# Row skewness of a 1024 x 8192 array: fixed engine orders, new column widths and slices, moved copies and closing steps

## The chip, the cores and the metric

The kernel runs on one core of one Trainium2 chip. The metric is the device time of one execution in microseconds (us). The core has a matrix engine (TensorE, PE in the profile, with PEld for its weight loads), a vector engine (VectorE, DVE), a scalar engine (ScalarE, ACT), GpSimd (POOL) and SyncE (SP), which here only issues the transfers. Each engine runs its own list of instructions in order, and waits on semaphores for the others.

## The reference

```python
rows, cols = 1024, 8192            # x is float32, standard normal
mean = np.mean(x, axis=-1, keepdims=True)
std = np.std(x, axis=-1, keepdims=True)
z = (x - mean) / (std + 1e-8)
return np.mean(z ** 3, axis=-1).astype(np.float32)
```

For each row the third standardised moment is wanted. Both kernels get it from three sums over the row, of x, x^2 and x^3: with m1, m2, m3 the means of these, var = m2 - m1^2 and skew = (m3 - 3 m1 m2 + 2 m1^3) * var^-1.5.

## The kernel before

The 1024 rows are eight blocks of 128 partitions (block b takes rows p*8+b). A block of 8192 columns is cut into units, one load each; `UNITS` lists their widths block by block. The loads are issued by SP in the order of the units, through a pool of eight buffers (`xp`, tag `x`), so load i+8 waits until unit i has been used by every engine.

A unit is cut into slices of at most `SUB_MAX` = 2304 columns (`_slices`). For each slice:

- ScalarE squares it (L147, scale 8192^-0.5) into a tile `sq` and sums the squares into a column of `s2u`.
- VectorE multiplies `sq` by x (L152), and sums the cubes into a column of `s3u`. Four buffers of `sq` rotate.
- For the last unit of the last block the squares go to PSUM (`sqps`) and the products to `cube`.

Sums of x go by TensorE: each 128 x 128 piece of the unit is multiplied with an identity and accumulated into one PSUM tile `tp` (L165). At the end of the block ScalarE copies `tp` to SBUF (`tsb`, L174), and one product with a vector of ones (L175) gives the means in a column of `s1ps`. In blocks 0 to 2 ScalarE sums 1024 of the columns itself (L159).

Closing: after block 5, `close_first_blocks` computes skew of blocks 0 to 5, with two reductions on VectorE (L99), four small steps on ScalarE and six on GpSimd (L110 to L115). For blocks 6 and 7, `close_on_act` does it on ScalarE: it sums the block's columns of `s2u` there (L123), takes m1^2, the variance, -3 m1 and their product (L124 to L128), and puts the correction into a spare column of `s3u`. Its steps for block 6 stand between the first Squares of block 7. At the very end GpSimd raises both variances to -1.5 (L187), VectorE reduces the columns of `s3u` of both blocks (L189), multiplies (L192), and SP stores `skew` (L193).

The order of the instructions on each engine is set by a scheduler from the program, and here it follows the order in which they are written, but for a few small steps of the closings, which it puts elsewhere.

Of the kernel before, what the change touches and what calls it, by code (L numbers as in the profile page):

```python
# [8 lines left out]
FP = mybir.dt.float32  # L9
AF = mybir.ActivationFunctionType  # L10
ALU = mybir.AluOpType
X_AXIS = mybir.AxisListType.X


UNITS = [
    [4096, 4096],
    [4096, 4096],
    [4096, 4096],
    [4096, 4096],
    [3584, 2304, 2304],  # L20
    [2304, 2304, 2048, 1536],
    [1664, 1792, 1920, 1664, 1152],
    [1024, 1024, 1152, 1280, 1408, 1152, 1152],
]
S1_ACT = {(0, 0): 1024, (1, 0): 1024, (2, 0): 1024}
SUB_MAX = 2304
X_BUFS = 8
SQ_BUFS = 4
EARLY = 6


def _slices(w):
    n = -(-w // SUB_MAX)
    step = -(-w // n // 128) * 128
    return [(s, min(s + step, w)) for s in range(0, w, step)]


@with_exitstack
def kernel(
    ctx: ExitStack,  # L40
    tc: tile.TileContext,
    x: bass.AP,
    out: bass.AP,
):
    nc = tc.nc
    P = nc.NUM_PARTITIONS
    R, C = x.shape
    NB = R // P
    L = NB - 1
    F = EARLY  # L50
    inv_n = 1.0 / float(C)
    s_scale = float(C) ** -0.5
    third = (1.0 / 3.0) ** 0.5
    assert len(UNITS) == NB and all(sum(u) == C for u in UNITS)
    nw = len(S1_ACT)
    assert sorted(b for b, _ in S1_ACT) == list(range(nw)) and nw <= F


    xv = x.rearrange("(p b) c -> b p c", b=NB)
    ov = out.rearrange("(p b) -> p b", b=NB)  # L60


    K = max(sum(len(_slices(w)) for w in u) for u in UNITS) + 1

    xpool = ctx.enter_context(tc.tile_pool(name="xp", bufs=X_BUFS))
    sqpool = ctx.enter_context(tc.tile_pool(name="sqp", bufs=SQ_BUFS))
    onep = ctx.enter_context(tc.tile_pool(name="onep", bufs=1))
    psum = ctx.enter_context(tc.tile_pool(name="ps", bufs=2, space=bass.MemoryType.PSUM))
    psum1 = ctx.enter_context(tc.tile_pool(name="ps1", bufs=1, space=bass.MemoryType.PSUM))

    def small(name, n):
        return onep.tile([P, n], FP, tag=name, name=name)

    onesn = small("onesn", 1)
    nc.vector.memset(onesn, inv_n)  # L75
    tiny = small("tiny", 1)
    nc.scalar.activation(out=tiny, in_=onesn, func=AF.Square)  # L77
    ident = small("ident", P)
    make_identity(nc, ident)
    s2u = small("s2u", NB * K)  # L80
    s3u = small("s3u", NB * K)
    nc.vector.memset(s2u, 0.0)
    nc.vector.memset(s3u, 0.0)
    s1a = small("s1a", nw)
    same = small("same", max(S1_ACT.values()))
    junk = small("junk", K)
    expo = small("expo", F)
    nc.gpsimd.memset(expo, -1.5)
    skew = small("skew", NB)
    s1ps = psum1.tile([P, NB], FP, tag="s1ps")  # L90
    m1a = small("m1a", F)
    var2 = small("var2", NB - F)
    Tsb = [small(f"tsb{i}", P) for i in range(2)]

    def close_first_blocks():

        m2, m3 = small("m2a", F), small("m3a", F)
        for dst, src in ((m2, s2u), (m3, s3u)):
            nc.vector.tensor_reduce(  # L99
                out=dst, in_=src[:, 0 : F * K].rearrange("p (b c) -> p b c", c=K),  # L100
                axis=X_AXIS, op=ALU.add,
            )
        m1sq, m1sq3, nm1 = small("m1sqa", F), small("m1sq3a", F), small("nm1a", F)
        nc.scalar.copy(out=m1a[:, nw:F], in_=s1ps[:, nw:F])
        nc.scalar.activation(out=m1sq, in_=m1a, func=AF.Square)
        nc.scalar.activation(out=m1sq3, in_=m1a, func=AF.Square, scale=third)
        nc.scalar.activation(out=nm1, in_=m1a, func=AF.Copy, scale=-3.0)
        g = nc.gpsimd
        var, rr = small("vara", F), small("rra", F)
        g.tensor_tensor(out=var, in0=m2, in1=m1sq, op=ALU.subtract)  # L110
        g.tensor_tensor(out=m1sq3, in0=m1sq3, in1=var, op=ALU.add)  # L111
        g.tensor_tensor(out=m1sq3, in0=m1sq3, in1=nm1, op=ALU.mult)  # L112
        g.tensor_tensor(out=m3, in0=m3, in1=m1sq3, op=ALU.add)  # L113
        g.tensor_tensor(out=rr, in0=var, in1=expo, op=ALU.pow)  # L114
        g.tensor_tensor(out=skew[:, 0:F], in0=m3, in1=rr, op=ALU.mult)  # L115

    def close_on_act(b):

        m2, m1sq, nm1, v3 = (small(f"{t}_{b}", 1) for t in ("m2", "m1sq", "nm1", "v3"))
        p1 = s1ps[:, b : b + 1]  # L120
        var = var2[:, b - F : b - F + 1]
        act = nc.scalar.activation
        yield act(out=junk, in_=s2u[:, b * K : b * K + K], func=AF.Copy, accum_out=m2)  # L123
        yield act(out=m1sq, in_=p1, func=AF.Square)  # L124
        yield act(out=var, in_=m1sq, func=AF.Identity, scale=-1.0, bias=m2)  # L125
        yield act(out=nm1, in_=p1, func=AF.Copy, scale=-3.0)  # L126
        yield act(out=v3, in_=m1sq, func=AF.Identity, scale=1.0 / 3.0, bias=var)  # L127
        yield act(  # L128
            out=s3u[:, b * K + K - 1 : b * K + K], in_=v3, func=AF.Identity, scale=nm1
        )  # L130

    pending = iter(())
    for b, widths in enumerate(UNITS):
        tp = psum.tile([P, P], FP, tag="tp", name=f"tp_{b}")
        c0 = 0
        j = b * K
        for k, w in enumerate(widths):
            last_unit = b == L and k == len(widths) - 1
            xt = xpool.tile([P, w], FP, tag="x", name=f"x_{b}_{k}")
            nc.sync.dma_start(out=xt, in_=xv[b, :, c0 : c0 + w])  # L140
            c0 += w
            for s, e in _slices(w):
                if last_unit:
                    sq = psum1.tile([P, e - s], FP, tag="sqps", name=f"sqps_{s}")
                else:
                    sq = sqpool.tile([P, e - s], FP, tag="sq", name=f"sq_{b}_{k}_{s}")
                nc.scalar.activation(  # L147
                    out=sq, in_=xt[:, s:e], func=AF.Square, scale=s_scale,
                    accum_out=s2u[:, j : j + 1],
                )  # L150
                cube = sqpool.tile([P, e - s], FP, tag="sq", name="cube") if last_unit else sq
                nc.vector.scalar_tensor_tensor(  # L152
                    out=cube, in0=sq, scalar=1.0, in1=xt[:, s:e],
                    op0=ALU.mult, op1=ALU.mult, accum_out=s3u[:, j : j + 1],
                )
                j += 1
            w_act = S1_ACT.get((b, k), 0)
            if w_act:
                nc.scalar.activation(  # L159
                    out=same[:, 0:w_act], in_=xt[:, w - w_act : w], func=AF.Copy,  # L160
                    scale=inv_n, accum_out=s1a[:, b : b + 1],
                )
            n = (w - w_act) // P
            for c in range(n):
                nc.tensor.matmul(  # L165
                    out=tp, lhsT=xt[:, c * P : (c + 1) * P], rhs=ident,
                    start=(k == 0 and c == 0), stop=(c0 == C and c == n - 1),
                    is_transpose=True,
                )
            if k > 0:  # L170
                next(pending, None)
                next(pending, None)
        tsb = Tsb[b % 2]
        nc.scalar.copy(out=tsb, in_=tp)  # L174
        nc.tensor.matmul(out=s1ps[:, b : b + 1], lhsT=tsb, rhs=onesn, start=True, stop=True)  # L175
        if b == F - 2:
            nc.vector.tensor_tensor(
                out=m1a[:, 0:nw], in0=s1ps[:, 0:nw], in1=s1a, op=ALU.add
            )
        if b == F - 1:  # L180
            close_first_blocks()
        if b >= F:
            pending = close_on_act(b)
    for _ in pending:
        pass
    rr = small("rr2", NB - F)
    nc.gpsimd.tensor_tensor(out=rr, in0=var2, in1=expo[:, 0 : NB - F], op=ALU.pow)  # L187
    num = small("num2", NB - F)
    nc.vector.tensor_reduce(  # L189
        out=num, in_=s3u[:, F * K :].rearrange("p (b c) -> p b c", c=K), axis=X_AXIS, op=ALU.add  # L190
    )
    nc.vector.tensor_tensor(out=skew[:, F:NB], in0=num, in1=rr, op=ALU.mult)  # L192
    nc.sync.dma_start(out=ov, in_=skew)  # L193


# [28 lines left out]
```

## Time and profile before

| | |
|---|---|
| median of 8 runs | 91.67 us (91.54 to 91.89) |
| the profiled execution, its own time | 91.63 us |
| its span, first to last instruction | 89.9 us |
| busy: VectorE, ScalarE, PE, GpSimd | 72.9, 72.1, 64.5, 10.3 us |
| data read | 33.55 MB, 373 GB/s over the span |
| loads of x | 27, of 512 KB to 2 MB |

The profile is of one execution. In strips, a digit is the busy share in tenths of one of 40 equal slices of the span. In the chain, the columns are start, length, and what ran, with "issue" for time in which nothing that is shown was waited for. Rows of the timeline give start, length, engine, line, operation, output <- inputs, shapes, count, and in brackets the idle time before and what ended it. A wait's numbers are the total, how often, and the longest.

### The profile page before, as it was taken

To read this page: it belongs to the slowest core of one execution; us is meant where nothing else is said; L and a number is where in the kernel's file an instruction comes from. 1 tells how busy PE (TensorE), PEld (TensorE's weight loads), DVE (VectorE), ACT (ScalarE), POOL (GpSimd) and SP (SyncE) were. 2 spreads that over 40 slices of the span, in tenths; PEclk is the share of its full clock that TensorE was granted. 3 is DMA by queue.
4 is the path that set the end of the run, shared out by engine and by line. 5 is a ranking of instruction groups with operands and counts; after the bars stand their busy time and mean duration, and the time that the engine had idled before them with its cause. 6 is when DMAs were issued, how large, how long until landed. Compare 5 with 4: busy or idle time off the path is not lost.

```text
span 89.9 us, 1368 instructions
## 1 busy us (share of the span) xinstructions
PE 64.5 (72%) x504; PEld 58.7 (65%) x504; DVE 72.9 (81%) x80; ACT 72.1 (80%) x106; POOL 10.3 (11%) x14
## 2 busy tenths in 40 slices
PE   0002999692898919889598988888988798969710
PEld 0003999591896909778596977877876786848500
DVE  1000498989989298998989999999999999999970
ACT  6003999699991999979598989978979898999950
POOL 3000000000000000000000000000005999400030
PEclk9999999999669999999999999999999999999995
DMA  4899999999999999999999999999999999994000
GB/s 117 328 394 452 445 423 416 445 430 416 452 423 408 445 430 408 445 430 423 428 397 422 414 435 410 419 419 420 413 410 420 407 409 417 421 409 173 0 0 2
DMA packets 4038, 33.64 MB, mean 374 GB/s; under 512 B 576, under 2 KB 576, under 8 KB 2240
## 3 DMA queue, kind: packets, MB, share of 16 engines
q1 hardware_dynamic: 4032, 33.56, 89.8%
q8 instruction: 4, 0.07, 0.3%
q14 instruction: 2, 0.02, 0.0%
HBM read 33.55 MB, written 0.00 MB: 373 GB/s over the span
## 4 chain that ended last, share of the span: by engine, by line
DMA 74%; ACT 15%; issue 4%; DVE 2%; SPq 1%; PE 1%; ACTq 0%; DVEq 0%
DMA x<-in_x_dram 74%; ACT sq L147 11%; ACT sqps L147 1%; DVE sq L152 1%; ACT same L159 1%; SPq L140 1%; PE s1ps L175 1%; ACT tsb L174 0%; ACT s3u L128 0%; ACT v L127 0%; ACT var L125 0%; DVE num L189 0%; ACT m1sq L124 0%; DVE skew L192 0%; ACT nm L126 0%
## 5 line engine op out<-in xcount | busy, mean ns | idle before, releaser
L152 DVE SCALAR_TENSOR_TENSOR sq<-sq,x 128x2048 f32<-128x2048 f32 (+9 forms) x35 | 70.8, 2071 | 13.3 <-ACT sq L147 13.2
L165 PE MATMUL tp<-ident,x 128*128 128x128 f32 x488 | 62.0, 286 | 17.8 <-DMA x<-in_x_dram 17.6
L165 PEld LDWEIGHTS tp<-ident,x 128*128 128x128 f32 x488 | 57.0, 149 | 21.6 <-DMA x<-in_x_dram 13.1
L147 ACT ACTIVATE sq<-x 128x2048 f32<-128x2048 f32 (+9 forms) x35 | 60.6, 1733 | 11.4 <-DMA x<-in_x_dram 11.3
L110 POOL TENSOR_TENSOR vara<-m2a,m1sqa 128x6 f32<-128x6 f32 x1 | 1.8, 1825 | 67.0 <-DVE m3a L99 67.0
L147 ACT ACTIVATION_READ_ACCUMULATOR sq<-x 128x1 f32 x35 | 6.5, 185 | 0.0
L175 PEld LDWEIGHTS s1ps<-onesn,tsb 128*128 128x128 f32 x16 | 2.4, 188 | 5.3 <-ACT tsb L174 5.3
L175 PE MATMUL s1ps<-onesn,tsb 128*128 128x1 f32 x16 | 3.1, 260 | 3.4 <-ACT tsb L174 3.4
L174 ACT COPY tsb<-tp 128x128 f32<-128x128 f32 x8 | 2.0, 253 | 1.5 <-PE tp L165 1.5
L159 ACT ACTIVATE same<-x 128x1024 f32<-128x1024 f32 x3 | 3.1, 1041 | 0.0
L152 DVE DVE_READ_ACCUMULATOR sq<-sq,x 128x1 f32 x35 | 2.9, 82 | 0.0
L111 POOL TENSOR_TENSOR m1sq3a<-m1sq3a,vara 128x6 f32<-128x6 f32 x1 | 1.9, 1867 | 0.1
L77 ACT ACT_TABLE_LOAD x1 | 1.3, 1283 | 0.7 <-PEq L208 0.7
L113 POOL TENSOR_TENSOR m3a<-m3a,m1sq3a 128x6 f32<-128x6 f32 x1 | 1.7, 1737 | 0.1
L187 POOL TENSOR_TENSOR rr<-var,expo 128x2 f32<-128x2 f32 x1 | 0.7, 700 | 8.8 <-ACT var L125 8.8
L152 DVE SCALAR_TENSOR_TENSOR cube<-sqps,x 128x1152 f32<-128x1152 f32 x1 | 1.4, 1351 | 0.0
L114 POOL TENSOR_TENSOR rra<-vara,expo 128x6 f32<-128x6 f32 x1 | 1.3, 1333 | 0.0
L115 POOL TENSOR_TENSOR skew<-m3a,rra 128x6 f32<-128x6 f32 x1 | 1.2, 1198 | 0.1
L147 ACT ACTIVATE sqps<-x 128x1152 f32<-128x1152 f32 x1 | 1.1, 1137 | 0.1
L112 POOL TENSOR_TENSOR m1sq3a<-m1sq3a,nm1a 128x6 f32<-128x6 f32 x1 | 1.0, 981 | 0.0
L124 ACT ACTIVATE m1sq<-s1ps 128x1 f32<-128x1 f32 x2 | 0.3, 171 | 0.5 <-PE s1ps L175 0.5
L75 DVE MEMSET onesn<- 128x1 f32 x1 | 0.1, 59 | 0.8 <-PEq L208 0.8
(28 smaller groups left out, 6.7 us busy)
## 6 DMA issues: line engine op xcount, KB each, us to landing
x<-in_x_dram SPq DMA_DIRECT2D x8, 2048.0 KB, 23.5
x<-in_x_dram SPq DMA_DIRECT2D x4, 1152.0 KB, 27.9
x<-in_x_dram SPq DMA_DIRECT2D x4, 576.0 KB, 8.7
x<-in_x_dram SPq DMA_DIRECT2D x1, 1792.0 KB, 33.0
x<-in_x_dram SPq DMA_DIRECT2D x2, 832.0 KB, 14.1
x<-in_x_dram SPq DMA_DIRECT2D x1, 1024.0 KB, 21.1
x<-in_x_dram SPq DMA_DIRECT2D x2, 512.0 KB, 10.2
x<-in_x_dram SPq DMA_DIRECT2D x1, 960.0 KB, 13.4
```

What stands on the lines that cost most here:

```text
L77: nc.scalar.activation(out=tiny, in_=onesn, func=AF.Square)
L110: g.tensor_tensor(out=var, in0=m2, in1=m1sq, op=ALU.subtract)
L111: g.tensor_tensor(out=m1sq3, in0=m1sq3, in1=var, op=ALU.add)
L113: g.tensor_tensor(out=m3, in0=m3, in1=m1sq3, op=ALU.add)
L114: g.tensor_tensor(out=rr, in0=var, in1=expo, op=ALU.pow)
L115: g.tensor_tensor(out=skew[:, 0:F], in0=m3, in1=rr, op=ALU.mult)
L147: nc.scalar.activation(out=sq, in_=xt[:, s:e], func=AF.Square, scale=s_scale, accum_out=s2u[:, j : j + 1],)
L152: nc.vector.scalar_tensor_tensor(out=cube, in0=sq, scalar=1.0, in1=xt[:, s:e], op0=ALU.mult, op1=ALU.mult, accum_out=s3u[:, j : j + 1],)
L159: nc.scalar.activation(out=same[:, 0:w_act], in_=xt[:, w - w_act : w], func=AF.Copy, scale=inv_n, accum_out=s1a[:, b : b + 1],)
L165: nc.tensor.matmul(out=tp, lhsT=xt[:, c * P : (c + 1) * P], rhs=ident, start=(k == 0 and c == 0), stop=(c0 == C and c == n - 1), is_transp ...
L174: nc.scalar.copy(out=tsb, in_=tp)
L175: nc.tensor.matmul(out=s1ps[:, b : b + 1], lhsT=tsb, rhs=onesn, start=True, stop=True)
```

## The change

- The engines' instruction orders are those in which the program is written, for all five engines (a manual schedule).
- Units of 3584 columns and more, from block 2 on, are cut into three slices of at most 1408.
- The widths of blocks 4 to 7 are new; the last unit has 896 columns instead of 1152. There are 27 loads before and after.
- The copy of `tp` and the product with ones of block b stand behind the first unit of block b+1 (`copy_sums`, `mean`), those of block 7 at the end.
- Steps are hung behind units by `at(block, unit, step)`: the first blocks' closing behind block 6, units 1 and 2; that of block 6 behind units 2, 3 and 4 of block 7, with VectorE doing its two reductions, ScalarE `third_1` and `third_2`, GpSimd the rest.
- At the end ScalarE sums all of block 7's `s2u`, and its `s3u` but for the last column; GpSimd computes the variance and its power; one VectorE step (`tensor_scalar`) adds the last column and multiplies.

```diff
-    [3584, 2304, 2304],
-    [2304, 2304, 2048, 1536],
-    [1664, 1792, 1920, 1664, 1152],
-    [1024, 1024, 1152, 1280, 1408, 1152, 1152],
+    [3072, 2944, 2176],
+    [2944, 2688, 2560],
+    [1664, 1536, 1664, 1792, 1536],
+    [1024, 1152, 768, 1024, 1024, 1280, 1024, 896],
 ]
+SUB_WIDE = 1408
+WIDE = 3584
-def _slices(w):
-    n = -(-w // SUB_MAX)
+def _slices(b, w):
+    n = -(-w // (SUB_WIDE if b >= 2 and w >= WIDE else SUB_MAX))
...
+    ctx.enter_context(tc.manual_schedule(
+        engines={eng.PE, eng.Activation, eng.DVE, eng.Pool, eng.SP}))
...
+    def copy_sums(b):
+        nc.scalar.copy(out=Tsb[b % 2], in_=tps[b])
+
+    def mean(b):
+        nc.tensor.matmul(
+            out=s1ps[:, b : b + 1], lhsT=Tsb[b % 2], rhs=onesn, start=True, stop=True
+        )
+
+    for b in range(L):
+        at(b + 1, 0, lambda b=b: copy_sums(b))
+        at(b + 1, 0, lambda b=b: mean(b))
...
+    at(F - 2, 0, lambda: v.tensor_tensor(
+        out=m1a[:, 0:nw], in0=s1ps[:, 0:nw], in1=s1a, op=ALU.add))
+    at(F, 1, first_sums)
+    at(F, 2, first_rest)
...
+    def mid_sums():
+        for t, src in (("m2", s2u), ("m3", s3u)):
+            v.tensor_reduce(
+                out=mid[t], in_=src[:, F * K : F * K + n_sl[F]], axis=X_AXIS, op=ALU.add
+            )
+        act(out=mid["m1sq"], in_=s1ps[:, F : F + 1], func=AF.Square)
+        act(out=mid["nm1"], in_=s1ps[:, F : F + 1], func=AF.Copy, scale=-3.0)
+        g.tensor_tensor(out=mid["var"], in0=mid["m2"], in1=mid["m1sq"], op=ALU.subtract)
+        g.tensor_tensor(out=mid["rr"], in0=mid["var"], in1=expo[:, 0:1], op=ALU.pow)
+
+    def third_1(o):
+        act(out=o["v3"], in_=o["m1sq"], func=AF.Identity, scale=-2.0 / 3.0, bias=o["m2"])
+
+    def third_2(o):
+        act(out=o["t"], in_=o["v3"], func=AF.Identity, scale=o["nm1"], bias=o["m3"])
+
+    at(L, 2, mid_sums)
+    at(L, 3, lambda: third_1(mid))
+    at(L, 4, lambda: third_2(mid))
+    at(L, 4, lambda: g.tensor_tensor(
+        out=skew[:, F : F + 1], in0=mid["t"], in1=mid["rr"], op=ALU.mult))
...
+            for fn in todo.pop((b, k), ()):
+                fn()
...
+    copy_sums(L)
+    row_sum(o["m2"], s2u, n_sl[L])
+    mean(L)
+    act(out=o["m1sq"], in_=p1, func=AF.Square)
+    g.tensor_tensor(out=o["var"], in0=o["m2"], in1=o["m1sq"], op=ALU.subtract)
+    g.tensor_tensor(out=o["rr"], in0=o["var"], in1=expo[:, 0:1], op=ALU.pow)
+    act(out=o["nm1"], in_=p1, func=AF.Copy, scale=-3.0)
+    third_1(o)
+    row_sum(o["m3"], s3u, n_sl[L] - 1)
+    third_2(o)
+    v.tensor_scalar(
+        out=skew[:, L:NB], in0=s3u[:, j - 1 : j], scalar1=o["t"], scalar2=o["rr"],
+        op0=ALU.add, op1=ALU.mult,
+    )
```

Here F is 6, L is 7, and `row_sum` is a Copy on ScalarE with an accumulated sum. GpSimd's closing of the first blocks now takes the power right after the variance. The order of the instructions on each engine in the built program is that of the text: on ScalarE, in block 7, `m1sq` and `nm1` of block 6 behind the Square of unit 2, `third_1` behind that of unit 3, `third_2` behind that of unit 4.

## The prediction

> **What bounds the kernel now.** I read the busy strips first, then the chain that ended last in order of time, then the timeline of the last 30 us.
>
> ```profile
> DMA  4899999999999999999999999999999999994000
> GB/s 117 328 394 452 445 423 416 445 430 416 452 423 408 445 430 408 445 430 423 428 397 422 414 435 410 419 419 420 413 410 420 407 409 417 421 409 173 0 0 2
> ```
>
> The DMA engines are busy from the second slice until the input has landed, and move about 420 GB/s in every slice between. Next, is anything upstream of them late? SP's own waits say no:
>
> ```profile
> SPq L140 <- DVE sq L152: 64.2, 19, 10.0
> ```
>
> SP waits 64.2 us for VectorE to free buffers, yet the transfers never run dry: eight buffers are in flight, and the shortest time from an issue to its landing is 7.5 us. So the stream of x is the bound, and only what follows its end can be shortened:
>
> ```profile
> 76.18 7.51 DMA x<-in_x_dram
> ...
> 83.71 1.26 ACT sqps L147 x2
> ...
> 84.97 0.27 ACT tsb L174
> ...
> 85.29 0.40 PE s1ps L175 x2
> ...
> 85.71 0.17 ACT m1sq L124
> ...
> 86.56 0.30 ACT s3u L128
> ...
> 86.89 0.18 DVE num L189
> ...
> 87.17 0.16 DVE skew L192
> ```
>
> The last unit lands at 83.69 and skew is complete at 87.33. The span ends at 89.9, 2.57 later (the store), and 1.73 more lie outside it (91.63 for this execution). The median of the runs is 91.67, so 0.04 is added at the end. The durations for the sum are in the timeline:
>
> ```profile
> 67.98 0.20 DVE L99 TENSOR_REDUCE m2a<-s2u 128x6 f32<-128x48 f32 x1
> ...
> 72.06 1.33 POOL L114 TENSOR_TENSOR rra<-vara,expo 128x6 f32<-128x6 f32 x1
> ...
> 74.22 1.89 DVE L152 SCALAR_TENSOR_TENSOR sq<-sq,x 128x1664 f32<-128x1664 f32 x1
> 74.43 1.74 POOL L113 TENSOR_TENSOR m3a<-m3a,m1sq3a 128x6 f32<-128x6 f32 x1
> ...
> 77.16 0.29 ACT L127 ACTIVATE v<-m1sq,var 128x1 f32<-128x1 f32 x1
> ...
> 77.36 1.04 ACT L147 ACTIVATE sq<-x 128x1024 f32<-128x1024 f32 x1
> ...
> 78.31 0.19 ACT L147 ACTIVATION_READ_ACCUMULATOR sq<-x 128x1 f32 x1
> ...
> 78.53 1.23 DVE L152 SCALAR_TENSOR_TENSOR sq<-sq,x 128x1024 f32<-128x1024 f32 x1
> ...
> 80.95 1.18 PEld L165 LDWEIGHTS tp<-ident,x 128*128 128x128 f32 x11 [0.67 <-DMA x<-in_x_dram]
> ...
> 82.36 0.96 PEld L165 LDWEIGHTS tp<-ident,x 128*128 128x128 f32 x9 [0.23 <-DMA x<-in_x_dram]
> ...
> 85.38 1.35 DVE L152 SCALAR_TENSOR_TENSOR cube<-sqps,x 128x1152 f32<-128x1152 f32 x1
> 86.28 0.70 POOL L187 TENSOR_TENSOR rr<-var,expo 128x2 f32<-128x2 f32 x1 [8.84 <-ACT var L125]
> ```
>
> The rules that I take from it. A 1024 Square occupies ScalarE for 1.04 (0.83 ns per column and 0.19), its sum is out 0.10 later, VectorE starts 0.03 after that, and needs 1.15 (1/0.96 ns per column and 0.08). The first transposes on PE show landings: 1.41 apart for 1152 columns, 4.90 for 4096 (33.90 to 38.80 on PE's rows); a line through them is 0.05 and 1.19 ns per column.
>
> **The stream.** Before and after, 27 loads carry the same bytes, so the sum of their steps is equal and the end stays at 83.69. The buffers stay ahead: by the rules above, even the last load is issued over 5 us before the one ahead of it lands. The first issues and the start are untouched: nothing.
>
> Here a rule speaks against the change. The row: 576 KB loads land 1.41 apart, 418 GB/s, against 2 MB in 4.90, 428 GB/s. The Trainium skill ("DMA: Bandwidth & Descriptors", section "Bandwidth") asks for transfers of at least 1 MiB and gives 341 GB/s at that size; by it the last load, now 448 KB, would take an estimated 1.35 instead of the 1.12 of my line, and the end would come some 0.2 later. That table is of single transfers; the trace has a full queue, so I use the row.
>
> **Three slices, even widths, copies moved, early closing.** Wide units of blocks 2 and 3 get one slice more, four in all, and other new widths bring another four: 8 × 0.19 on ScalarE, 8 × 0.08 on VectorE. A 4096 unit then takes VectorE 3 × 0.08 + 4.27 = 4.5 of the 4.9 that its load takes, so the stream hides it; without that cover it would be 0.6. The copies behind the next block's first unit take away ScalarE's waits for PE (1.47 at 28.3), equally hidden: zero. PE's mean product waits behind 8 to 32 transposes, and its first user (block 5's mean) comes a whole unit later: zero. First-block sums on VectorE cost the same 0.23 as now.
>
> **The mid closing, where I see the loss.** In block 7 the order is fixed: after unit 2 VectorE reduces the sums of block 6, and after the Square of unit 3 ScalarE runs `third_1`, which needs the first of these sums. ScalarE can't pass it, and behind it are queued the Squares of units 4 to 7, for which VectorE waits. Before, ScalarE summed s2u itself and never waited for VectorE there. Working back from 83.69, landings are: unit 6 82.57, unit 5 81.30, 4 79.73, 3 78.46, and block 6 unit 3 at 71.66. From that landing, where VectorE has caught up (free at 73.35):
>
> - Square of 1792 from 71.74 to 73.52; VectorE 73.55 to 75.50; then, back to back, 1536, 1024, 1152 and 768 columns (1.68, 1.15, 1.28, 0.88): 80.49. The first sum is out at 80.69.
> - ScalarE has ended unit 3's Square at about 79.6 and unit 4 has landed; `third_1` starts at 80.75, a stall of 1.1. The next Square starts 0.20 later (as 77.16 to 77.36): 80.95.
> - From there ScalarE is late: unit 4 to 81.99, `third_2` 0.19, unit 5 from 82.18, 6 from 83.45, 7 from 84.49 (landed 83.69; now it starts at 83.71).
> - VectorE waits for unit 4 until 82.12 and unit 5 until 83.56, then runs 5, 6 and 7: 84.97, 86.12, 87.13; with the read of the accumulator 87.21, where it is 86.74 now.
>
> So the smaller last unit (0.21 of Square, 0.27 of cube) is more than given back.
>
> **The new end.** The copy starts at 85.43 (84.97 now) and the last mean's Square 0.74 later as now, 86.17. ScalarE: `third_1` at 86.37, the sum of s3u, `third_2`, out at 87.13. GpSimd: two operations in a row, where now there is one. Subtract starts at 86.42 (0.08 after ScalarE, as 86.28 was). Its price on [128,1] is in no row: at least the 0.13 by which arithmetic on GpSimd ends after a VectorE step (76.17 against 76.03), at most the 0.70 of pow; I take 0.30, nearest to the unobstructed rows (0.29 for the select at the start). Hand-over 0.08. Pow was 1.33 for six columns and 0.70 for two, a line that gives 0.54 for one; bounds 0.3 and 0.7. So 87.34, and VectorE's last step starts 0.06 later, takes 0.16 (bounds 0.1 to 0.25), ends at 87.56 against 87.33. If GpSimd is quicker, cube at 87.21 is the floor: 87.41.
>
> Sum: +0.23, floor +0.08; with 0.70 for each GpSimd step +0.8. I round to 0.25: 91.63 + 0.25 = 91.88, with 0.04 91.92.
>
> The second weighing is here. Five arithmetic operations on GpSimd end 0.13 after a VectorE step with both operands in SBUF (74.43 + 1.74 against 74.22 + 1.81): they wait for it. Cube reads sqps from PSUM, and pow at 86.28 ended 0.32 after cube: no clear sign. The Trainium skill ("GPSIMD Engine Reference", section "1. Specifications") names two SBUF inputs as what contends, so cube should not hold the subtract; by it the sum is the one above, and without it that of the second rival.
>
> **Rivals.**
> - *The stall is not there (faster).* If VectorE is through unit 2 about half a us earlier than I work out, or the wait falls before the landing of unit 4, VectorE runs back to back from unit 3 (80.72) to 86.67, ends at 86.87, −0.46: 91.2. The point: `third_1` must start before 80.2. For it: VectorE had no backlog at 79.86 in the trace. Against: ScalarE had itself been slowed there by closing block 6. 15%.
> - *GpSimd is held by cube (slower).* The subtract ends 0.13 after 87.13, pow follows, 87.88; with the last step 88.1: +0.8, 92.5. It decides if a step with one PSUM operand holds GpSimd's port. 13%.
> - *Nothing shows.* The stall and the shorter end cancel, VectorE's floor of +0.08 holds: 91.75. This is the low part of my forecast, 25%.
>
> **The numbers.** My forecast, stall and an end at +0.08 to +0.5, has 70%; what is over, 2%, is landings that shift. About 0.2%, 0.18 us, is what a measurement here can tell from no change. Of the 70%, 25 lie below that; so faster 0.15, same 0.25, slower 0.60. The range leaves out most of the faster rival, reaches half way to it (a stall half as long), takes in the GpSimd bounds and the second rival: 91.45 to 92.55.
>
> **What would show it.** Right: last landing near 83.7; ScalarE idle about 1.1 before `third_1` of block 6, released by VectorE's reduce; last Square from about 84.5 though landed earlier; cube through at 87.2; two GpSimd steps in a row ahead of the last step. Wrong: `third_1` without idle time before it; the last Square at once after the landing; a GpSimd subtract over 0.7; a landing moved by over 0.3.

## The result, and the profile after

The changed kernel takes 92.03 us (median of 10 runs, 91.98 to 92.18), the kernel before 91.67: a ratio of 1.0042, 95% interval 1.0034 to 1.0050. It is slower by 0.36 us, twice the 0.18 that counts as a change here. Its profiled execution took 92.16, 0.13 over its median, with a span of 90.3.

I read the same views as of the kernel before. First, two lines of the page: the strip of the DMA engines and the shares of the chain that ended last:

```profile
DMA  4899999999999999999999999999999999992000
...
DMA 44%; DVE 28%; issue 11%; ACT 10%; SPq 4%; PE 0%; DVEq 0%; ACTq 0%
```

Before, 74% of this chain was DMA. Now VectorE has 28% of it: followed back from the end, the chain leaves the stream at 43.84 and runs through VectorE's products. The stream itself is as it was: the strip has no gap before its end, and the last landing is near 83.7 (PE's row for it, below, is at 83.74; before it was at 83.73). The last 7 us of the chain in order of time (start, length, what ran) show where the end is made:

```profile
80.55 0.08 DVE sq L193
80.63 0.15 DVE m L154 x2
80.78 0.02 issue
80.80 0.10 ACT v L163
80.89 0.11 issue
81.00 1.13 ACT sq L188 x2
82.13 0.28 ACT t L166
82.41 2.29 ACT sq L188 x4
84.70 0.93 ACT sqps L188 x2
...
86.98 0.40 ACT t L166
...
87.50 0.27 DVE skew L231
```

Before, the chain went from the landing at 83.69 straight into the last Square. Now it passes from a VectorE reduction (L154) to ScalarE's `third_1` (`v`, L163), and then through every Square of units 4 to 7 without a gap. The timeline gives the details:

```profile
79.88 0.86 PEld L206 LDWEIGHTS tp<-ident,x 128*128 128x128 f32 x8 [0.43 <-DMA x<-in_x_dram]
...
80.80 0.29 ACT L163 ACTIVATE v<-m1sq,m 128x1 f32<-128x1 f32 x1 [1.01 <-DVE m L154]
...
83.74 0.75 PEld L206 LDWEIGHTS tp<-ident,x 128*128 128x128 f32 x7 [0.19 <-DMA x<-in_x_dram]
...
84.61 0.90 ACT L188 ACTIVATE sqps<-x 128x896 f32<-128x896 f32 x1
...
86.26 1.08 DVE L193 SCALAR_TENSOR_TENSOR cube<-sqps,x 128x896 f32<-128x896 f32 x1
...
86.51 0.19 POOL L225 TENSOR_TENSOR var<-m,m1sq 128x1 f32<-128x1 f32 x1 [3.07 <-ACT nm L227]
...
86.77 0.54 POOL L226 TENSOR_TENSOR rr<-var,expo 128x1 f32<-128x1 f32 x1
86.98 0.39 ACT L166 ACTIVATE t<-v,m,nm 128x1 f32<-128x1 f32 x1
87.27 0.08 DVE L193 DVE_READ_ACCUMULATOR cube<-sqps,x 128x1 f32 x1
87.50 0.27 DVE L231 TENSOR_SCALAR skew<-s3u,t,rr 128x1 f32<-128x1 f32 x1
```

PE's rows with a DMA as releaser are the landings: unit 4 at 79.88, the last unit at 83.74. ScalarE idles 1.01 in front of `third_1` though unit 4 is there, and starts the last Square 0.9 after its unit has landed. Three chains then end together: t at 87.37, cube's sum at 87.35, the power at 87.31. `skew` is complete at 87.77, 0.44 after the 87.33 of before.

### The profile page after: what moved, and what is told of

The parts are those of the page before. It is cut to its first block, busy times and chain, and to the rows that moved or that the text cites. A ratio compares the mean times of both kernels' runs of the same rounds, so it can differ in the third digit from the quotient of the medians.

```text
span 90.3 us, 1403 instructions
## 1 busy us (share of the span) xinstructions
PE 66.1 (73%) x504; PEld 62.1 (69%) x504; DVE 73.6 (82%) x97; ACT 72.5 (80%) x120; POOL 12.5 (14%) x18
## 4 chain that ended last, share of the span: by engine, by line
DMA 44%; DVE 28%; issue 11%; ACT 10%; SPq 4%; PE 0%; DVEq 0%; ACTq 0%
DMA x<-in_x_dram 44%; DVE sq L193 27%; ACT sq L188 7%; SPq L181 4%; ACT sqps L188 1%; ACT t L166 1%; PE s1ps L111 0%; ACT v L163 0%; DVE skew L231 0%; ACT junk L219 0%; ACT m1sq L224 0%; ACT tsb L108 0%; DVE m L154 0%; DVE m3a L126 0%; DVE m2a L126 0%
## 5 line engine op out<-in xcount | busy, mean ns | idle before, releaser
L193 DVE SCALAR_TENSOR_TENSOR sq<-sq,x 128x1408 f32<-128x1408 f32 (+9 forms) x43 | 71.8, 1720 | 13.2 <-ACT sq L188 13.1
L206 PE MATMUL tp<-ident,x 128*128 128x128 f32 x488 | 64.3, 295 | 12.6 <-DMA x<-in_x_dram 12.5
L188 ACT ACTIVATE sq<-x 128x1408 f32<-128x1408 f32 (+9 forms) x43 | 62.3, 1451 | 12.8 <-DMA x<-in_x_dram 12.3
L206 PEld LDWEIGHTS tp<-ident,x 128*128 128x128 f32 x488 | 60.8, 155 | 15.1 <-issue 8.2
L188 ACT ACTIVATION_READ_ACCUMULATOR sq<-x 128x1 f32 x43 | 8.0, 186 | 0.0
L133 POOL TENSOR_TENSOR rra<-vara,expo 128x6 f32<-128x6 f32 x1 | 3.2, 3171 | 0.1
L163 ACT ACTIVATE v<-m1sq,m 128x1 f32<-128x1 f32 x2 | 0.6, 295 | 1.0 <-DVE m L154 1.0
L159 POOL TENSOR_TENSOR var<-m,m1sq 128x1 f32<-128x1 f32 x1 | 1.1, 1101 | 0.2 <-DVE m L154 0.2
L193 DVE SCALAR_TENSOR_TENSOR cube<-sqps,x 128x896 f32<-128x896 f32 x1 | 1.1, 1085 | 0.0
L188 ACT ACTIVATE sqps<-x 128x896 f32<-128x896 f32 x1 | 0.9, 898 | 0.0
L171 POOL TENSOR_TENSOR skew<-t,rr 128x1 f32<-128x1 f32 x1 | 0.8, 787 | 0.1
```

What stands on the lines that cost most here:

```text
L133: g.tensor_tensor(out=rra, in0=vara, in1=expo, op=ALU.pow)
L188: act(out=sq, in_=xt[:, s:e], func=AF.Square, scale=s_scale, accum_out=s2u[:, j : j + 1],)
L193: v.scalar_tensor_tensor(out=cube, in0=sq, scalar=1.0, in1=xt[:, s:e], op0=ALU.mult, op1=ALU.mult, accum_out=s3u[:, j : j + 1],)
L206: nc.tensor.matmul(out=tp, lhsT=xt[:, c * P : (c + 1) * P], rhs=ident, start=(k == 0 and c == 0), stop=(c0 == C and c == n - 1), is_transp ...
```

## The experiments

The theory: the loss is ScalarE's wait for VectorE in `third_1` and the Squares queued behind it. The rivals: it lies in the new end, or in VectorE's extra work. Ratios are to the kernel before, measured beside each.

**The steps moved by one unit.**

```diff
-    at(L, 3, lambda: third_1(mid))
-    at(L, 4, lambda: third_2(mid))
-    at(L, 4, lambda: g.tensor_tensor(
+    at(L, 4, lambda: third_1(mid))
+    at(L, 5, lambda: third_2(mid))
+    at(L, 5, lambda: g.tensor_tensor(
```

> The changed kernel with block 6's third_1 behind unit 4 of block 7 (was 3) and third_2 with its GpSimd product behind unit 5 (was 4); nothing else. Theory (the loss is ScalarE's 1.01 us stall in third_1, behind which the Squares of units 4 to 7 are queued): the sum is there when third_1 comes up, no stall; the last Square starts at its landing, 83.7, instead of 84.61; VectorE runs back to back from 80.68 and ends cube at about 86.6; end of skew about 87.0 against 87.77, so about 0.75 us less than the changed kernel, some 91.3, faster than the kernel before (91.67) by 0.4. Rival (the loss lies in the new end, or in VectorE's work, not in the place of third_1): within 0.15 of the changed kernel, 91.9 to 92.2.

Measured: 91.36, ratio 0.9965 (0.9953 to 0.9978), 0.67 less than the changed kernel. Its timeline:

```profile
80.95 0.28 ACT L163 ACTIVATE v<-m1sq,m 128x1 f32<-128x1 f32 x1
...
82.69 0.37 ACT L166 ACTIVATE t<-v,m,nm 128x1 f32<-128x1 f32 x1
...
84.01 0.90 ACT L188 ACTIVATE sqps<-x 128x896 f32<-128x896 f32 x1
...
86.87 0.27 DVE L231 TENSOR_SCALAR skew<-s3u,t,rr 128x1 f32<-128x1 f32 x1 [0.27 <-ACT t L166]
```

`third_1` has no idle time before it; it runs right behind unit 4's Square. The last Square starts 0.60 earlier and the last step 0.63. Moving three steps turns a kernel slower than before into a faster one, so the new end and VectorE's work are not the loss. The last Square was expected at 83.7 and started at 84.01: `third_2` (0.37, of which 0.28 pass before the next Square starts) now stands between units 5 and 6, where ScalarE has no time to spare.

**The place kept, the wait taken away.**

```diff
-        for t, src in (("m2", s2u), ("m3", s3u)):
-            v.tensor_reduce(out=mid[t], ...)
+        v.tensor_reduce(out=mid["m3"], in_=s3u[:, F * K : F * K + n_sl[F]], ...)
+        act(out=junk[:, 0 : n_sl[F]], in_=s2u[:, F * K : F * K + n_sl[F]],
+            func=AF.Copy, accum_out=mid["m2"])
```

> The changed kernel with third_1 and third_2 where they are, but the sum of block 6's squares taken on ScalarE (a Copy with accumulation, right before m1sq) instead of VectorE; VectorE keeps only the reduction of the cubes. Theory (it is the wait for VectorE that costs, not the place of the steps): third_1 waits for nothing of VectorE, ScalarE pays 0.3 once and catches up by the landing of unit 5; last Square at 83.8, end about 0.7 less than the changed kernel, some 91.3. Rival (the steps between the Squares are what delays them): no gain, 92.0 to 92.3, since ScalarE has 0.3 more to do.

Measured: 91.27, ratio 0.9956 (0.9943 to 0.9968). In its timeline:

```profile
79.69 0.28 ACT L166 ACTIVATE v<-m1sq,m 128x1 f32<-128x1 f32 x1
...
83.79 0.90 ACT L191 ACTIVATE sqps<-x 128x896 f32<-128x896 f32 x1
...
86.26 0.39 ACT L169 ACTIVATE t<-v,m,nm 128x1 f32<-128x1 f32 x1
86.45 0.09 DVE L196 DVE_READ_ACCUMULATOR cube<-sqps,x 128x1 f32 x1
86.74 0.27 DVE L234 TENSOR_SCALAR skew<-s3u,t,rr 128x1 f32<-128x1 f32 x1 [0.21 <-ACT t L169]
```

The steps stand between the same Squares as in the changed kernel, and ScalarE has one step more to run. Yet the end comes 0.76 earlier. It was the wait for VectorE, not the steps. VectorE has one reduction less here, but that is worth only 0.07: in the changed kernel the two start at 80.55 and 80.62.

**Two slices again in blocks 2 and 3** (`SUB_WIDE` 2304 for 1408).

> The changed kernel with the units of 4096 in blocks 2 and 3 in two slices of 2048 again instead of three. Theory (the stream hides it): within 0.1 of the changed kernel; the last landing stays at 83.7. Rival (the 4 x 0.08 on VectorE and 4 x 0.19 on ScalarE reach the end): 0.3 to 0.6 less. Rival (earlier slices free buffers earlier and help): 0.1 to 0.5 more.

Measured: 92.20, ratio 1.0058 (1.0045 to 1.0071), 0.17 more than the changed kernel; the intervals overlap, so the time alone doesn't settle it. The last landing has hardly moved (PE's row for it is at 83.70, for 83.74). VectorE's rows in the timeline of this kernel, and after them the same rows of the changed one:

```profile
71.69 0.20 DVE L126 TENSOR_REDUCE m2a<-s2u 128x6 f32<-128x48 f32 x1
...
73.72 2.03 DVE L193 SCALAR_TENSOR_TENSOR sq<-sq,x 128x1792 f32<-128x1792 f32 x1
```

```profile
71.43 0.20 DVE L126 TENSOR_REDUCE m2a<-s2u 128x6 f32<-128x48 f32 x1
...
73.62 2.02 DVE L193 SCALAR_TENSOR_TENSOR sq<-sq,x 128x1792 f32<-128x1792 f32 x1
```

In a unit of 4096 columns VectorE starts 2.04 after ScalarE's first Square with two slices (38.83 to 40.87), and 1.51 after it with three (39.02 to 40.53). With two it is 0.26 later at the reduction, carries 0.10 of this past a short gap, and ends 0.10 later (skew at 87.87). The time lies in the range of the second rival, but not for its reason: buffers that come free earlier would show in the landings, and the last one did not come later. The rows suggest that the slices help a little, through VectorE's backlog. That this reaches the time is not shown: the 0.10 compares two single executions, whose own times are 92.17 and 92.16.

**The last squares in SBUF instead of PSUM.**

```diff
-                    sq = psum1.tile([P, e - s], FP, tag="sqps", name="sqps")
+                    sq = sqpool.tile([P, e - s], FP, tag="sq", name="sqps")
```

> The changed kernel with the last unit's squares in SBUF instead of PSUM, so that the last product reads two operands in SBUF. Theory (GpSimd waits for a VectorE step with two SBUF operands, not for one with a PSUM operand): the subtract at 86.5 is held until 0.13 after the last product's end, 87.4; pow follows to 88.0, the last VectorE step ends at about 88.35 instead of 87.77: 0.55 more than the changed kernel, some 92.6. Rival (GpSimd is not held by this, and the 0.19 of the subtract says nothing of PSUM): within 0.15 of the changed kernel.

Measured: 92.56, ratio 1.0099 (1.0083 to 1.0114), 0.53 more. In its timeline:

```profile
86.10 1.09 DVE L193 SCALAR_TENSOR_TENSOR cube<-sqps,x 128x896 f32<-128x896 f32 x1
...
86.34 0.89 POOL L225 TENSOR_TENSOR var<-m,m1sq 128x1 f32<-128x1 f32 x1 [3.07 <-ACT nm L227]
...
87.11 0.09 DVE L193 DVE_READ_ACCUMULATOR cube<-sqps,x 128x1 f32 x1
87.31 0.54 POOL L226 TENSOR_TENSOR rr<-var,expo 128x1 f32<-128x1 f32 x1
87.89 0.27 DVE L231 TENSOR_SCALAR skew<-s3u,t,rr 128x1 f32<-128x1 f32 x1 [0.70 <-POOL rr L226]
```

The same subtract takes 0.89 instead of 0.19 and ends at 87.23, 0.12 after the read of cube's accumulator starts (87.11). Here one operand's place decides whether GpSimd is held.

**The old widths of blocks 4 to 7, without the stall.** Only `UNITS` is put back, in the second experiment's kernel.

> The kernel with block 6's squares summed on ScalarE (no stall), with the widths of blocks 4 to 7 of the kernel before. It asks what the widths are worth once the stall is gone. Theory (the widths matter only by the last unit, 1152 for 896 columns): the last Square starts at its landing, 83.72, PE's last transposes end at 84.95, the copy starts there and the last step on ScalarE is out at about 86.8 instead of 86.65; end 0.15 to 0.2 later than without the old widths, some 91.45. Rival (even widths matter for VectorE's backlog all along): 0.4 or more later, 91.7 or above.

Measured: 91.51, ratio 0.9988 (0.9980 to 0.9997). That is 0.24 more than with the new widths, or 0.29 by the ratios: a little above the theory's 0.15 to 0.2, and below its rival's 0.4. In its timeline:

```profile
81.14 0.96 PEld L209 LDWEIGHTS tp<-ident,x 128*128 128x128 f32 x9 [0.66 <-DMA x<-in_x_dram]
...
81.18 1.38 ACT L191 ACTIVATE sq<-x 128x1408 f32<-128x1408 f32 x1 [0.18 <-DVE sq L196]
...
83.92 0.96 PEld L209 LDWEIGHTS tp<-ident,x 128*128 128x128 f32 x9 [0.42 <-DMA x<-in_x_dram]
...
83.98 1.12 ACT L191 ACTIVATE sqps<-x 128x1152 f32<-128x1152 f32 x1
...
87.11 0.27 DVE L234 TENSOR_SCALAR skew<-s3u,t,rr 128x1 f32<-128x1 f32 x1 [0.23 <-ACT t L169]
```

The end is 0.37 later than with the new widths (87.11 for 86.74), but this execution is the slowest of its eleven, 91.67, and its stream is late: PE's row for the last landing is at 83.92, for 83.78 in the second experiment and 83.73 in the kernel before, which has these widths. So some 0.14 of the 0.37 can be the stream's. The last Square itself takes 0.22 longer (1.12 for 0.90), about the 0.21 of 256 columns at 0.83 ns. The two together are about the 0.37, but no run shows where this kernel ends with an earlier stream. The Square of 1408 columns shows a wait of 0.18 that VectorE ended, but its unit had landed only some 0.04 before (PE's row at 81.14), so in this execution VectorE's backlog cost little there. What the medians show beyond the last unit's 0.21, under 0.1, stays open. Against the kernel before this version gains only 0.0012 of the time, some 0.11 us, where the second experiment gains 0.40: most of what is gained without the stall comes with the widths.

**The copies behind their own block again** (`at(b, len(UNITS[b]) - 1, ...)` for `copy_sums` and `mean`, in the same kernel).

> The same kernel without the stall (block 6's squares summed on ScalarE), with copy_sums and mean of each block behind the block's own last unit, as in the kernel before. Theory (ScalarE's waits for PE are covered: VectorE has its backlog): within 0.1 of 91.27, though ScalarE waits up to 1 us for PE at block ends. Rival (the move pays): 0.2 to 0.8 later.

Measured: 91.35, ratio 0.9967 (0.9956 to 0.9979); not to be told from 91.27. The waits of this kernel (total, times, longest) have a line that the changed kernel's have not:

```profile
ACT tsb L108 <- PE tp L209: 2.9, 3, 1.5
```

ScalarE waits 2.9 us for PE, and none of it shows in the time.

**The written order alone**, the four lines of the manual schedule put into the kernel before.

> The kernel before with the engines' orders as written and nothing else. Theory (the scheduler had kept the written order but for a few small closing steps): within 0.1 of 91.67. Rival (the order of those steps matters): 0.2 or more either way.

Measured: 91.70, ratio 1.0000 (0.9988 to 1.0011). Nothing.

**A last unit of 768 columns, without the stall** (block 7 as 1024, 1152, 1024, 1024, 1024, 1152, 1024, 768).

> The kernel without the stall (block 6's squares summed on ScalarE), block 7 in widths 1024, 1152, 1024, 1024, 1024, 1152, 1024, 768. ScalarE's closing chain (out at 86.65) and cube (read out at 86.54) end together there; a last unit of 768 takes 0.1 from the former, while VectorE's total of columns stays. Theory (both chains bound the end): 0.0 to 0.1 less, 91.17 to 91.27. Rival (only ScalarE's chain from the last landing bounds it): 0.1 to 0.15 less.

Measured: 91.24, ratio 0.9955 (0.9943 to 0.9967), the same as 91.27 within the measurement, which is too coarse to tell the theory from its rival. By the trace t is out at 86.52 for 86.65, and cube's sum at 86.52 for 86.54: VectorE's end hardly moves, as the theory says, and the last step starts 0.08 earlier (86.66). The two versions without the stall, at 896 and 768 columns, are the best measured; both beat the kernel before by some 0.45%.

## Why the prediction was right

**The stream.** Forecast to end at 83.69, as before; it ended there within 0.05. The rule of large transfers would have put it 0.2 later; here a last load of 448 KB has its row on PE at 83.74, and one of 576 KB before had it at 83.73, so with a full queue the smaller loads cost nothing that shows.

**Slices, copies, written order.** Each was put at zero. The written order is nothing (1.0000), and the moved copies show nothing (91.35 for 91.27). The slices may not quite be: the price looked at was their 8 × 0.08 on VectorE. What was missed is that VectorE, started 0.53 earlier in each unit of 4096, carries a smaller backlog from block 3 on; by two single traces 0.10 of it is left at the end.

**The mid closing.** This step decided it, and its numbers came out nearly one for one: first sum out at 80.69 (measured 80.70), `third_1` at 80.75 (80.80), stall 1.1 (1.01), last Square at 84.49 (84.61), cube's sum at 87.21 (87.35). One size was off: `third_2` holds the next Square back for 0.28 (82.04 to 82.32), where 0.19 was forecast, most of the 0.12 by which the last Square was later. The first two experiments show the wait to be the cause: without it the kernel is at 91.36 and 91.27, near the 91.2 of the faster rival, which described the change without a stall.

**The new end.** Forecast 87.56, measured 87.77. The steps are those of the forecast, but three sizes in it were off, and so was the path. GpSimd's subtract took 0.19, not 0.30; the pow exactly 0.54. So the power, forecast to be the last of the three chains at 87.34, was out first, at 87.31. `third_2` took 0.39 for 0.29. The rows of ScalarE's small steps are 0.17 for m1sq, which has no per-partition scalar operand, 0.30 for `v` with one, and 0.39 for t with two; the row that I used, `v`, has only one. The Trainium skill ("ScalarE: Activation LUTs", section "What ACT_TABLE_LOAD costs") adds about 93 ns for each per-partition scalar operand, and the rows agree. With the late last Square this put t at 87.37 where 87.13 was forecast, 0.02 behind cube's sum and 0.06 behind GpSimd's power: ScalarE's t was the end. The last VectorE step took 0.27 for 0.16, just over its bound of 0.25. It reads two scalars from memory, and the row it was sized by reads none; whether that is the reason no run here tests.

**The GpSimd rival** fell for this kernel and was right as a mechanism one operand away. The subtract took 0.19 beside a product with a PSUM operand, and 0.89 in the fourth experiment, beside one with both in SBUF. The rule of the Trainium skill ("GPSIMD Engine Reference", section "1. Specifications"), that two SBUF inputs contend, agrees with these rows.

**The total.** 91.92 forecast, 92.03 measured. The cause was right, but the total is nearer than the working. The profiled executions, from which the sum was made, stand 0.53 apart (92.16 and 91.63), where 0.25 was forecast; 0.44 of it lies ahead of the store, for the 0.23 of the forecast. The medians are only 0.36 apart because the changed kernel's profiled execution lies 0.13 above its median, and the other 0.04 below. That the forecast met the median within 0.11 is in part luck.

## What to carry to other kernels

A step that is moved from an engine with slack to one with a backlog brings that backlog back as a wait, and everything that the waiting engine has in its list is delayed with it: before hanging such a step behind a unit, work out when the producer gets there, not when its input lands. Here one unit later, or the sum on the engine that needs it, was worth 0.7 us. When a stream is the bound, an engine that is only a little faster than it (here VectorE, 4.51 us for a unit of 4096 columns that lands every 4.90) can still have a backlog at the end of the stream, and delays far back in the kernel may show there.

## What the runs showed of the hardware

- GpSimd's subtract on [128,1] took 0.19 beside a VectorE product with one operand in PSUM, and 0.89 beside the same product with both operands in SBUF. The pow on [128,1] took 0.54 when it was not held.
- The six-column pow took 1.33 in the kernel before, where it started 0.07 ahead of a product with both operands in SBUF, and 3.17 in the changed one, where it started 0.05 behind the start of one that ran for 1.95.
- ScalarE's small steps took 0.17, 0.30 and 0.39 with none, one and two scalars read from memory.
